# The affine step of the attention residual, moved from POOL in the output projection to DVE beside the projection of the values

## The chip, the cores and the metric

The kernel runs on one core of one Trainium2 chip. The metric is device time of that core in microseconds, from start to end of one execution; it is given as the median of several runs. Five engines matter: PE (TensorE, matmuls and transposes), DVE (VectorE), ACT (ScalarE), POOL (GpSimd) and SP (SyncE, which issues nearly all DMAs here). Each engine works through its own instructions in the order in which they stand.

## The reference

A trunk of two layers over 1024 tokens of width 1024. Layer 0 mixes with a state space model (`s5_mixer`), layer 1 with dilated attention; behind each mixer stand a residual with layer norm, a gated feed-forward network with a short convolution, and another residual with layer norm. The keys and values of the attention are projected from the output of layer 0.

```
def post_norm(x, f, gain, bias):
    return layer_norm(DN_ALPHA * x + f.astype(x.dtype), gain, bias)

for layer in range(DEPTH):
    mix = s5_mixer(h, ...) if layer < N_A_LAYERS else dilated_attention(h, w_q, w_out, rel_bias, kv_blocks)
    h = post_norm(h, mix, ln_gain[layer, 0], ln_bias[layer, 0])
    ffn = conv_glu_ffn(h, ffn_w_up[layer], ...)
    h = post_norm(h, ffn, ln_gain[layer, 1], ln_bias[layer, 1])
    if layer == N_A_LAYERS - 1:
        kv_blocks = shared_kv(h, attn_w_kv)
```

What is changed is where a part of one line is computed: the `* gain + bias` of the norm that ends layer 0, and the `DN_ALPHA *` of the residual that ends the attention. The attention reads `h` in another form, transposed, and gets gain and bias there by another way; the residual reads it token by token.

## The kernel before, in words

All matrices are in fp32 and each product is made of three matmuls (lines 88 to 90: high times high, high times low, low times high). For that every operand is split into a high part, by a cast on ACT (line 83, `CAST wh`, `CAST hT`), and a low part, by a subtraction on DVE (line 84, `wl`, `hT`). A weight tile is 128x1024 fp32 (512 KB): SP loads it into one of two buffers named `raw` (line 75), ACT and DVE split it into `wh` and `wl`.

A tensor of 1024x1024 is held as eight tiles `acc` of 128 tokens by 1024. At the end of layer 0 the function `after` normalizes each tile (line 129, mean and deviation only) and stores it to DRAM as `h1` (line 1556, `h<-acc` in the profile). For the matmuls the same tiles are transposed: `to_T` and `turn` let PE transpose blocks into PSUM (line 180, `tp`), and ACT (line 185) or DVE (line 183) write `tmp`, the block times gain plus bias, which is then split into `hT`. The tokens come in two halves, `hT[k][0]` and `hT[k][1]`, k from 0 to 7.

Then the values are projected. `values_first` does the first block for the token tiles j = 0 to 3, with the first half of `hT`, while PE still lacks the second. Behind it stand the transposes of the second half, and then, in `attention`, the same block for j = 4 to 7 and five more blocks. In `attention` the pool `ap` is opened, on memory that the tiles of layer 0 (`acc`, `tmp`, the weights of the values) held. For the first block, two of its four pairs of weights (k = 0 to 3) are kept from before; the other two (k = 4 to 7) are split anew into tiles of `ap`. The matmuls of these tiles are `v<-wh,hT` in the profile, and the copies of their results `vs<-v` (line 529), stored to `vscr`.

Behind the attention stands the output projection, `out_proj`, which is used by both layers. It takes the tokens in groups of three, three and two tiles; for each group it runs through eight weight tiles `in_w_out`. Before the matmuls of layer 1, SP loads two tiles `gb` (gain and bias, one row of DRAM broadcast to 128 partitions, line 156) and the eight tiles `acc` back from `h1` (line 1543, `acc<-h`). POOL multiplies each by the gain and adds the bias (lines 134 and 135). When a group's matmuls are done, DVE computes ALPHA times `acc` plus the product in PSUM (line 1489, `acc<-acc,wo`), and the norm follows.

A scheduler sets the order of the instructions on each engine, from its own forecast of their times. It works for the whole program but the state space model, so that a change at one place also moves instructions at others. A tile in a newly opened pool waits for all that used the memory under it.

Of the kernel before, what the change touches and what calls it, by code (L numbers as in the profile page):

```python
# [13 lines left out]
ALU = mybir.AluOpType  # L14
# [4 lines left out]
P = 128  # L19
# [5 lines left out]
ALPHA = (2.0 * 2) ** 0.25  # L25
# [448 lines left out]
def attn_bias_rows(net, pool, ps1):  # L474

    nc, a = net.nc, net.a
    rb = net.cp.tile([64, NG, 32], F32, "rb")
    nc.gpsimd.memset(rb[:], 0.0)
    nc.gpsimd.memset(rb[32:64], -1e30)
    for g in range(NG):  # L480
        nc.sync.dma_start(rb[0:32, g, 0:16], a["rel_bias"][:, g * 16 : g * 16 + 16])
    net.brow = net.dp.tile([NG, 16, LB], F32, name="brow")
    for g in range(NG):
        raw = pool.tile([P, 2, 512], F32, "s", "oh")
        nc.sync.dma_start(raw[0:64, 0, 0:LB], a["onehot"][:, g])
        ps = ps1.tile([P, 512], F32, "t", "bps")
        nc.tensor.matmul(ps[0:32, 0:LB], rb[:, g, :], raw[0:64, 0, 0:LB], start=True, stop=True)
        nc.scalar.copy(raw[0:16, 1, 0:LB], ps[0:16, 0:LB])
        nc.sync.dma_start(net.brow[g], raw[0:16, 1, 0:LB])


def attn_bias(net):

    net.bscr = []
    for g in range(NG):
        scr = net.dp.tile([16, P, LB], F32, name=f"bscr{g}")
        net.nc.gpsimd.dma_start(scr[:], net.brow[g].unsqueeze(1).broadcast_to([16, P, LB]))
        net.bscr.append(scr)
# [46 lines left out]
def attention(net, hT, ap, ws):  # L545
    nc = net.nc
    net.evn = 0
    for blk in range(2 * NG):
        if blk:
            ws = [net.wload(net.a["w_v"][blk, i], **({"pool": ap, "tag": "q"} if i < 3 else {})) for i in range(4)]  # L550
        else:
            ws = ws + [net.wload(net.a["w_v"][0, i], pool=ap, tag="q") for i in (2, 3)]
        for j in range(8) if blk else range(4, 8):
            ps = net.psA.tile([P, 512], F32, "mm", "v")
            st = ap.tile([P, 4, P], F32, "pt", "vs")
            value_tile(net, blk, j, hT, ws, ps[:], st[:])

    net.oscr = net.dp.tile([8, P, T], F32, name="oscr")
    nxt = Pair(net, 0, hT, ap)
    nxt.proj(0)  # L560
    for hp in range(8):
        pair = nxt
        for g in range(NG):
            if g:
                pair.proj(g)
            pair.scores(g)
        if hp < 7:
            nxt = Pair(net, hp + 1, hT, ap)
            nxt.proj(0)
        oT = pair.output()  # L570

    row = [[net.xp.tile([P, 2, 512], F32R, "x", "gT") for k in range(KT)] for _ in range(2)]
    for k in range(KT):
        if k < 7:
            raw = net.rawp.tile([P, T], F32, "raw", "oraw")
            nc.sync.dma_start(raw[:], net.oscr[k])
        else:
            raw = oT
        for hf in range(2):
            x = row[hf][k]  # L580
            net.split(raw[:, hf * 512 : hf * 512 + 512], x[:, 0, :], x[:, 1, :], nc.gpsimd if k < 7 else nc.vector)
    return [[row[hf][k] for hf in range(2)] for k in range(KT)]
# [885 lines left out]
    return gT  # L1468


def out_proj(net, w, gT, load, accp, hres, middle):

    nc = net.nc
    accs = []
    for tts in ((0, 1, 2), (3, 4, 5), (6, 7)):
        for tt in tts:
            accs.append(accp.tile([P, D], F32, "acc"))
            load(accs[tt], tt)
        pss = [net.psp.tile([P, D], F32, "mm", "wo") for _ in tts]
        for k in range(KT):  # L1480
            wh, wl = net.wload(w[k])
            for tt, ps in zip(tts, pss):
                g, q = gT[k][tt // 4], tt % 4
                lh, ll = (g[:, i, q * P : q * P + P] for i in range(2))
                for h in range(2):
                    sl = slice(h * 512, h * 512 + 512)
                    net.mm3(ps[:, sl], lh, ll, wh[:, sl], wl[:, sl], k == 0, k == KT - 1)
        for tt, ps in zip(tts, pss):
            nc.vector.scalar_tensor_tensor(
                out=accs[tt][:], in0=accs[tt][:], scalar=ALPHA, in1=ps[:], op0=ALU.mult, op1=ALU.add  # L1490
            )
            net.ln_apply(accs[tt])
            nc.sync.dma_start(hres[tt * P : tt * P + P, :], accs[tt][:])
        if 3 in tts:
            middle(accs)
    return accs


def program(tc, a, out):
    nc = tc.nc  # L1500
    with ExitStack() as ctx:
        net = Net(tc, ctx, a, out)
        net.persistent()
        net.dp = ctx.enter_context(tc.tile_pool(name="dp", bufs=1, space=DRAM))
        xp = net.xp = net.pool("xp", x=16)
        yT = [[None, None] for _ in range(KT)]
        with ExitStack() as c:
            cs = net.pool("s5c", c, c32=31, other=1)
            sp = net.pool("s5", c, s=11, w3=8, w2=3, u=3, Y=2, ms=2, r8=2, rq=1, other=1)
            psv, ps1 = net.pool("psv", c, PSUM, v=2), net.pool("ps1", c, PSUM, t=4)  # L1510
            s5 = S5(net, sp, cs, psv, ps1)
            s5.load_params()
            attn_bias_rows(net, sp, ps1)
            s5.run(xp, yT)

        net.weight_pools(4, 2)
        h1 = net.dp.tile([T, D], F32, name="h1")
        for l in range(2):
            if l == 1:
                with ExitStack() as c:  # L1520
                    gT = attention(net, hT, setup(net, c), V0)
            with ExitStack() as c:
                accp, tm = net.pool(f"acc{l}", c, acc=8), net.pool(f"tm{l}", c, t=4)
                hres = net.dp.tile([T, D], F32, name=f"hres{l}")
                half0 = []
                with ExitStack() as c2:
                    net.psp, net.tp = net.pool(f"ps{l}", c2, PSUM, mm=3, tp=2), "tp"
                    gp = net.pool(f"g{l}", c2, y=16)

                    def middle(accs):  # L1530
                        half0.extend(net.to_T(accs, 0, 2 * l, xp, tm))

                    if l == 0:
                        gT = glu(net, yT, tm, gp)
                        attn_bias(net)

                        def load(acc, tt):
                            nc.sync.dma_start(acc[:], a["x"][tt * P : tt * P + P, :])
                    else:
                        gb = net.load_gb(gp, 1, "y")  # L1540

                        def load(acc, tt):
                            nc.sync.dma_start(acc[:], h1[tt * P : tt * P + P, :])
                            net.ln_affine(acc, gb, nc.gpsimd)

                    accs = out_proj(net, a["w_out0" if l == 0 else "w_out1"], gT, load, accp, hres, middle)
                with ExitStack() as c2:
                    net.psp, net.tp = net.pool(f"pf{l}", c2, PSUM, s=6, tp=2), "tp"
                    fp = net.pool(f"f{l}", c2, xc=12, ws=5)
                    done, early = [], []  # L1550

                    def after(tt, acc):
                        done.append(acc)
                        if l == 0:
                            net.ln_apply(acc)
                            nc.sync.dma_start(h1[tt * P : tt * P + P, :], acc[:])
                            if tt == 4:
                                early.extend(net.to_T(done, 0, 1, xp, tm)[0])
                            return
                        if tt == 0:  # L1560
                            after.gb = net.load_gb(fp, 3, "xc")
                        net.ln_final(acc, after.gb, tt)
                        nc.sync.dma_start(out[tt * P : tt * P + P, :], acc[:])

                    net.ffn(l, accs, half0, xp, tm, fp, accp, hres, after)
                if l == 0:
                    with ExitStack() as c2:
                        net.psp, net.tp = net.pool("pv", c2, PSUM, mm=3, tp=2), "tp"
                        fp = net.pool("fv", c2, x=14)
                        hT = [[x, None] for x in early]  # L1570
                        V0 = values_first(net, hT, fp)
                        for k, t in enumerate(net.to_T(done, 1, 1, xp, tm)[0]):
                            hT[k][1] = t


def feature_tiles(w):
# [58 lines left out]
```

## Time and profile before

| | us |
|---|---|
| median of 3 runs (lowest, highest) | 3154.55 (3151.91, 3155.58) |
| the profiled execution | 3154.37 |
| its span, first to last instruction | 3152.4 |
| PE busy in the span | 2901.9 (92%) |
| DVE busy | 1929.7 (61%) |
| ACT busy | 1126.6 (36%) |
| POOL busy | 260.8 (8%) |

The profile is of one execution, and its places are given in us from the start of the span. The end of layer 0 and the first values lie at 1110 to 1180, the last pair of the attention and the output projection of layer 1 at 2200 to 2410. What lies outside the span is 3154.37 - 3152.4 = 2.0 us. PE is busy 92% of the span, so almost every wait of PE, and each stretch that it runs at a lower clock, is in the time.

### The profile page before, as it was taken

The numbers are of one execution on the slowest core, as the hardware profiler recorded it, in microseconds if no ns is written. First come the engines' busy times: TensorE is split into PE (matmuls) and PEld (weight loads), VectorE is DVE, ScalarE is ACT, GpSimd is POOL, SyncE is SP. The second block draws the span as 40 slices with busy tenths as digits, with TensorE's granted clock in tenths as the row PEclk, the third lists the DMA queues.
The fourth block names the chain that finished last, engine by engine and source line by source line (L and its number), as shares of the span: only waits on it lengthen the run. The fifth ranks groups of instructions, "written<-read, shape, count | busy, mean of one in ns | idle before, by whom it ended". The sixth has DMA issues, their size and how long they took to land.

```text
span 3152.4 us, 38280 instructions
## 1 busy us (share of the span) xinstructions
PE 2901.9 (92%) x13926; PEld 2374.7 (75%) x13926; DVE 1929.7 (61%) x3605; ACT 1126.6 (36%) x1977; POOL 260.8 (8%) x259
## 2 busy tenths in 40 slices
PE   4689989999989989999999999999688999998988
PEld 3668768888767768998777777777566788886766
DVE  8964687777688751113444444344457877767797
ACT  2433343333334431102433334333424433333442
POOL 8920000000100000000000000000250000001010
PEclk8889999999999999999999999999799999998999
DMA  5231532333653233326555556545443332328332
GB/s 176 59 122 60 174 104 105 112 109 112 249 179 107 89 102 113 107 68 164 148 151 146 134 140 156 141 130 144 137 170 137 111 107 107 107 101 336 98 101 67
DMA packets 189291, 408.11 MB, mean 129 GB/s; under 512 B 23984, under 2 KB 65696, under 8 KB 189104
## 3 DMA queue, kind: packets, MB, share of 16 engines
q1 hardware_dynamic: 180656, 373.16, 38.7%
q0 software_dynamic: 8448, 32.51, 2.8%
q8 instruction: 110, 1.80, 0.2%
q14 instruction: 77, 0.63, 0.1%
HBM read 249.79 MB, written 89.73 MB: 108 GB/s over the span
## 4 chain that ended last, share of the span: by engine, by line
PE 79%; DVE 8%; DMA 5%; POOL 4%; ACT 2%; issue 2%; SPq 1%; DVEq 0%; ACTq 0%; POOLq 0%
PE dn L398 13%; PE p L89 7%; PE p L88 7%; PE p L90 7%; PE qk L88 6%; PE qk L89 6%; PE qk L90 6%; PE o L810 3%; PE v L88 3%; PE v L90 3%; PE v L89 3%; PE t L800 2%; PE s L673 2%; DMA vs<-vs 1%; PE pa L88 1%
## 5 line engine op out<-in xcount | busy, mean ns | idle before, releaser
L398 PE MATMUL dn<-wh,ax 128*128 128x512 f32 x1408 | 396.5, 401 | 51.0 <-ACT ax L83 49.8
L84 DVE TENSOR_TENSOR wl<-raw,wh 128x1024 fp32r<-128x1024 f32 x174 | 221.7, 1275 | 280.8 <-ACT wh L83 280.7
L88 PE MATMUL p<-xc,wc 128*128 128x512 f32 x880 | 351.3, 400 | 16.6 <-DVE s L288 10.1
L83 ACT CAST wh<-raw 128x1024 fp32r<-128x1024 f32 x174 | 182.5, 1049 | 507.2 <-PE qk L89 155.1
L398 PEld LDWEIGHTS dn<-wh,ax 128*128 128x128 f32 x1408 | 269.0, 193 | 118.7 <-ACT ax L83 59.4
L90 PE MATMUL p<-xc,wc 128*128 128x512 f32 x880 | 348.1, 397 | 3.7 <-DVE wc L84 3.7
L89 PE MATMUL p<-xc,wc 128*128 128x512 f32 x880 | 351.2, 399 | 0.0
L88 PE MATMUL qk<-hT,wh 128*128 128x512 f32 x768 | 308.9, 402 | 10.4 <-DVE ql L611 10.4
L89 PE MATMUL qk<-hT,wh 128*128 128x512 f32 x768 | 308.5, 402 | 0.0
L90 PE MATMUL qk<-hT,wl 128*128 128x512 f32 x768 | 307.3, 400 | 0.0
L398 PE MATMUL dn<-wl,ax 128*128 128x512 f32 x704 | 228.9, 406 | 0.0
L88 PEld LDWEIGHTS p<-xc,wc 128*128 128x128 f32 x880 | 167.5, 190 | 60.2 <-ACT wc L83 20.5
L90 PEld LDWEIGHTS p<-xc,wc 128*128 128x128 f32 x880 | 166.3, 189 | 44.6 <-DVE wc L84 5.4
L89 PEld LDWEIGHTS p<-xc,wc 128*128 128x128 f32 x880 | 167.9, 191 | 39.3
L83 ACT CAST wc<-s 128x512 fp32r<-128x512 f32 x176 | 108.1, 621 | 238.6 <-PE p L90 228.9
L88 PEld LDWEIGHTS qk<-hT,wh 128*128 128x128 f32 x768 | 148.0, 193 | 41.7 <-DVE ql L611 12.4
L90 PEld LDWEIGHTS qk<-hT,wl 128*128 128x128 f32 x768 | 147.8, 192 | 29.7
L89 PEld LDWEIGHTS qk<-hT,wh 128*128 128x128 f32 x768 | 148.1, 193 | 28.9
L398 PEld LDWEIGHTS dn<-wl,ax 128*128 128x128 f32 x704 | 139.4, 198 | 31.4
L661 DVE CUSTOM_DVE_ANT_0 p<-s,bt 128x256 f32<-128x256 f32 (+1 forms) x384 | 119.2, 370 | 65.9 <-PE s L673 65.4
L88 PE MATMUL v<-wh,hT 128*128 128x512 f32 x384 | 153.7, 401 | 5.1 <-DVE tmp L183 4.8
L89 PE MATMUL v<-wl,hT 128*128 128x512 f32 x384 | 153.4, 400 | 0.0
(295 smaller groups left out, 5655.2 us busy)
## 6 DMA issues: line engine op xcount, KB each, us to landing
raw<-in_w_up SPq DMA_DIRECT2D x94, 512.0 KB, 3.5
qs<-qh SPq DMA_DIRECT2D x288, 128.0 KB, 2.4
vs<-vs SPq DMA_DIRECT2D x132, 256.0 KB, 3.5
raw<-in_w_out SPq DMA_DIRECT2D x48, 512.0 KB, 3.5
kl<-ql SPq DMA_DIRECT2D x192, 128.0 KB, 2.4
vs<-cv SPq DMA_DIRECT2D x44, 512.0 KB, 3.0
wd<-in_w_down POOLq DMA_DIRECT2D x44, 512.0 KB, 16.4
vs<-yv SPq DMA_DIRECT2D x38, 512.0 KB, 2.6
```

Of the source, the lines that this page charges most:

```text
L83: nc.scalar.copy(hi, x)
L84: (eng or nc.vector).tensor_tensor(out=lo, in0=x, in1=hi.bitcast(F32), op=ALU.subtract)
L88: nc.tensor.matmul(out, lh, rh, start=first, stop=False)
L89: nc.tensor.matmul(out, lh, rl, start=False, stop=False)
L90: nc.tensor.matmul(out, ll, rh, start=False, stop=last)
L398: nc.tensor.matmul(ps[i][h][:], l_, w[wi][:, h * 512 : h * 512 + 512], start=(f == 0 and l_ is ah and wi == 0), stop=(f == NF - 1 and l_ i ...
L661: nc.vector.tensor_tensor_reduce(out=out, in0=s, in1=b, scale=1.0, scalar=-3.0e38, op0=ALU.add, op1=ALU.max, accum_out=m)
L673: nc.tensor.matmul(out, qx[:, qs], kv[i], start=(i == 0), stop=(i == 1))
L800: nc.tensor.transpose(ps[:, i * P : i * P + P], b, net.ident[:])
L810: nc.tensor.matmul(o[64 * h : 64 * h + 64, oc], v[:, 64 * h : 64 * h + 64], pt[h], start=st, stop=sp_)
```

## The change: what it does

The affine step leaves `load` in the output projection, with its two loads of `gb`. It now stands at the end of layer 0, behind `values_first` and the transposes of the second half: gain and bias are loaded there, ACT multiplies both by ALPHA (2 instructions of 128x1024), DVE multiplies each of the eight `acc` tiles by the one and adds the other (16 instructions of 128x1024), and each tile is then stored to `h1`. The stores of `h1` that `after` made as soon as a tile was normalized go; their number, eight, stays. `out_proj` in layer 1 loads finished tiles and adds the product with a factor of 1.0 in place of ALPHA. The instruction on DVE there is the same.

```
-def out_proj(net, w, gT, load, accp, hres, middle):
+def out_proj(net, l, gT, load, accp, hres, middle):
     nc = net.nc
+    w = net.a[f"w_out{l}"]
...
             nc.vector.scalar_tensor_tensor(
-                out=accs[tt][:], in0=accs[tt][:], scalar=ALPHA, in1=ps[:], op0=ALU.mult, op1=ALU.add
+                out=accs[tt][:], in0=accs[tt][:], scalar=1.0 if l else ALPHA, in1=ps[:], op0=ALU.mult, op1=ALU.add
             )
...
-                        gb = net.load_gb(gp, 1, "y")
-
                         def load(acc, tt):
                             nc.sync.dma_start(acc[:], h1[tt * P : tt * P + P, :])
-                            net.ln_affine(acc, gb, nc.gpsimd)
-
-                    accs = out_proj(net, a["w_out0" if l == 0 else "w_out1"], gT, load, accp, hres, middle)
+
+                    accs = out_proj(net, l, gT, load, accp, hres, middle)
...
                         if l == 0:
                             net.ln_apply(acc)
-                            nc.sync.dma_start(h1[tt * P : tt * P + P, :], acc[:])
                             if tt == 4:
...
                         for k, t in enumerate(net.to_T(done, 1, 1, xp, tm)[0]):
                             hT[k][1] = t
+
+                        gb = net.load_gb(fp, 1)
+                        for g in gb:
+                            nc.scalar.mul(g[:], g[:], ALPHA)
+                        for tt, acc in enumerate(done):
+                            net.ln_affine(acc, gb, nc.vector)
+                            nc.sync.dma_start(h1[tt * P : tt * P + P, :], acc[:])
```

Where the scheduler put this shows in the built programs. The first place is DVE behind the first values, before the change: `tmp` are the transposed blocks of the second half, `hT` their low parts, and `wl` at the end the low part of the new weights for k = 4 and 5.

```order
L183 TENSOR_SCALAR tmp_8470<-tp_8480,lnT_59 128x512
L84 TENSOR_TENSOR hT_8469<-tmp_8470,hT_8469 128x512
L183 TENSOR_SCALAR tmp_8489<-tp_8499,lnT_59 128x512
L84 TENSOR_TENSOR hT_8479<-tmp_8470,hT_8479 128x512
L84 TENSOR_TENSOR hT_8488<-tmp_8489,hT_8488 128x512
L183 TENSOR_SCALAR tmp_8508<-tp_8518,lnT_59 128x512
L84 TENSOR_TENSOR hT_8498<-tmp_8489,hT_8498 128x512
L84 TENSOR_TENSOR hT_8507<-tmp_8508,hT_8507 128x512
L183 TENSOR_SCALAR tmp_8527<-tp_8537,lnT_59 128x512
L84 TENSOR_TENSOR hT_8517<-tmp_8508,hT_8517 128x512
L84 TENSOR_TENSOR hT_8526<-tmp_8527,hT_8526 128x512
L84 TENSOR_TENSOR hT_8536<-tmp_8527,hT_8536 128x512
```

After the change the same stretch of DVE begins with the same four instructions, and then goes on so, its middle and its end:

```order
L134 TENSOR_TENSOR acc_6469<-acc_6469,gb_8537 128x1024
L134 TENSOR_TENSOR acc_6555<-acc_6555,gb_8537 128x1024
L134 TENSOR_TENSOR acc_6641<-acc_6641,gb_8537 128x1024
L183 TENSOR_SCALAR tmp_8500<-tp_8510,lnT_59 128x512
L134 TENSOR_TENSOR acc_6727<-acc_6727,gb_8537 128x1024
...
L183 TENSOR_SCALAR tmp_8519<-tp_8529,lnT_59 128x512
L134 TENSOR_TENSOR acc_7673<-acc_7673,gb_8537 128x1024
...
L84 TENSOR_TENSOR hT_8528<-tmp_8519,hT_8528 128x512
L135 TENSOR_TENSOR acc_7673<-acc_7673,gb_8539 128x1024
L84 TENSOR_TENSOR wl_8593<-raw_8590,wh_8592 128x1024
```

All 16 affine instructions stand between the second split of `hT` (8471) and `wl`, the last one right before `wl`. Ten of them (seven multiplications, three additions) stand ahead of the last `tmp` (8519).

The second place is SP at the same time, after the change: the stores of the values, the loads of `gb`, the stores of `h1`, and the first loads of the attention behind them. Each store waits for DVE.

```order
L531 DMA vscr<-vs_8406 128x4x128 [waits DVE_49]
L156 DMA gb_8537<-in_ln 128x1024
L156 DMA gb_8539<-in_ln 128x1024
L531 DMA vscr<-vs_8434 128x4x128 [waits DMAHW3_49,Activation_49]
...
L1577 DMA h_1744<-acc_7410 128x1024 [waits DMAHW0_49,DVE_49]
L1577 DMA h_1744<-acc_7492 128x1024 [waits DMAHW1_49,DVE_49]
L1577 DMA h_1744<-acc_7591 128x1024 [waits DMAHW2_49,DVE_49]
L1577 DMA h_1744<-acc_7673 128x1024 [waits DMAHW3_49,DVE_49]
L873 DMA eye_1445_8583<-in_eye 128x128 [waits DMAHW4_49,DMAHW3_49,DMAHW5_49,DMAHW2_49,DMAHW6_49,DMAHW1_49,DMAHW7_49,DMAHW0_49,PE_49]
```

Before the change the eight stores of `h1` stood further up, among the loads for the feed-forward network and for the values. The third place is ACT at the cast of the new weights, after the change; DMAHW0 to DMAHW7 are the eight completion counters that SP's DMAs take in turn.

```order
L1574 ACTIVATE gb_8539<-gb_8539 128x1024 [waits DMAHW2_49]
L83 CAST hT_8499<-tmp_8500 128x512 [waits Activation_49]
L185 ACTIVATE tmp_8519<-tp_8520,lnT_59 128x512 [waits PE_49]
L83 CAST hT_8509<-tmp_8500 128x512 [waits DVE_49]
L83 CAST hT_8518<-tmp_8519 128x512 [waits Activation_49]
L83 CAST hT_8528<-tmp_8519 128x512 [waits DVE_49]
L83 CAST wh_8592<-raw_8590 128x1024 [waits DMAHW3_49,DMAHW2_49,DMAHW4_49,DMAHW1_49,DMAHW5_49,DMAHW0_49,DMAHW6_49,DVE_49,DMAHW7_49,PE_49,Activation_49]
```

The cast waits for counters of DMAs in both programs, for seven before and eight after. The counts that it waits for are those of DMAs on the memory of layer 0: before the change four stores of values and three of `h1`, which need nothing of the second half's splits; after it the eight stores of `h1`, the last of which waits for the last affine instruction (`acc_7673`). The order of PE in this stretch is the same as before.

## Rows read from the trace of the kernel before

**Rows 1.** The page's first part: busy us, share, instructions.

```profile
PE 2901.9 (92%) x13926; PEld 2374.7 (75%) x13926; DVE 1929.7 (61%) x3605; ACT 1126.6 (36%) x1977; POOL 260.8 (8%) x259
```

**Rows 2.** Stretches: length, busy us by engine (PE first), PE clock, DMA, GB/s.

```profile
1134.00:1180.00 46.00, 42.39 (x191) 34.09 (x191) 15.80 (x20) 14.17 (x20) 0.00 (x0) 0.96 0.38 116
...
2297.00:2320.00 23.00, 18.02 (x75) 14.27 (x75) 7.26 (x7) 5.33 (x6) 13.76 (x6) 0.96 0.71 274
...
2319.00:2322.00 3.00, 3.00 (x8) 1.99 (x8) 3.00 (x2) 0.81 (x1) 3.00 (x1) 0.50 0.33 53
...
2345.00:2350.00 5.00, 3.90 (x17) 3.21 (x18) 5.00 (x12) 2.08 (x6) 5.00 (x2) 1.00 0.39 105
```

**Rows 3.** Timeline of DVE at the first values: start, length, idle before.

```profile
1148.09 0.69 DVE L529 COPY vs<-v 128x512 f32<-128x512 f32 x1 [9.73 <-PE v L90]
...
1156.09 0.81 DVE L183 TENSOR_SCALAR tmp<-tp,lnT 128x512 f32<-128x512 f32 x1
1156.81 1.29 DVE L84 TENSOR_TENSOR hT<-tmp,hT 128x512 fp32r<-128x512 f32 x2
1158.01 0.81 DVE L183 TENSOR_SCALAR tmp<-tp,lnT 128x512 f32<-128x512 f32 x1
```

**Rows 4.** Timeline of PE at the values behind the transposes.

```profile
1160.89 0.66 PE L88 MATMUL v<-wh,hT 128*128 128x512 f32 x1 [1.25 <-DVE tmp L183]
...
1168.05 0.63 PE L88 MATMUL v<-wh,hT 128*128 128x512 f32 x2
1168.52 0.40 PE L89 MATMUL v<-wl,hT 128*128 128x512 f32 x1
...
1174.19 0.50 PE L88 MATMUL v<-wh,hT 128*128 128x512 f32 x1 [0.36 <-DVE vs L529]
```

**Rows 5.** Timeline of ACT there: a transposed block, the new weights.

```profile
1155.87 0.77 ACT L185 ACTIVATE tmp<-tp,lnT 128x512 f32<-128x512 f32 x1
...
1162.62 2.00 ACT L83 CAST wh<-raw 128x1024 fp32r<-128x1024 f32 x2 [1.11 <-DVE hT L84]
```

**Rows 6.** Timeline of DVE in layer 0's feed-forward network, an affine step.

```profile
870.24 2.35 DVE L134 TENSOR_TENSOR acc<-acc,gb 128x1024 f32<-128x1024 f32 x2
872.51 1.22 DVE L135 TENSOR_TENSOR acc<-acc,gb 128x1024 f32<-128x1024 f32 x1
```

**Rows 7.** Scaling of gb on ACT, by line: ns min, median, max.

```profile
L419 ACT ACTIVATE gb<-gb x4: 1058/1061/1062, 836.1 to 2852.2; 128x1024 f32<-128x1024 f32 x4
```

**Rows 8.** Landing of the eight stores of h1, line 1556.

```profile
DMA to landing us min/median/max: 2.6/2.9/6.6
```

**Rows 9.** Landing of the two loads of gb at 2299, line 156.

```profile
DMA to landing us min/median/max: 3.8/4.5/5.2
```

**Rows 10.** Timeline of SP at the output projection of layer 1.

```profile
2299.05 0.81 SPq L156 DMA_DIRECT2D gb<-in_ln  x2
2299.90 5.03 SPq L1543 DMA_DIRECT2D acc<-h  x8
```

**Rows 11.** The chain of waits there: start, length, what.

```profile
2306.10 11.30 DMA raw<-in_w_out
2317.49 1.05 ACT wh L83
```

**Rows 12.** Timeline of PE there, its waits.

```profile
2318.59 1.65 PE L88 MATMUL wo<-wh,gT 128*128 128x512 f32 x3 [4.92 <-ACT wh L83]
...
2339.28 0.47 PE L88 MATMUL wo<-wh,gT 128*128 128x512 f32 x1 [1.02 <-DVE acc L1489]
2346.10 0.50 PE L89 MATMUL wo<-wl,gT 128*128 128x512 f32 x1 [1.58 <-DVE wl L84]
2380.07 0.50 PE L89 MATMUL wo<-wl,gT 128*128 128x512 f32 x1 [1.82 <-DVE wl L84]
```

**Rows 13.** Groups by line, 1150 to 1176: busy us, mean ns, idle before.

```profile
L84 DVE TENSOR_TENSOR wl<-raw,wh 128x1024 fp32r<-128x1024 f32 x4 | 4.8, 1220 | 7.4 <-ACT wh L83 7.4
```

**Rows 14.** Groups by line, 2297 to 2350.

```profile
L84 DVE TENSOR_TENSOR wl<-raw,wh 128x1024 fp32r<-128x1024 f32 x9 | 19.9, 2224 | 23.4 <-ACT wh L83 23.4
```

## The prediction

> **What bounds the kernel now.** I read the page's busy times first, then the stretches, the timelines of PE, DVE, ACT and SP at the two places that the change touches, and last the chain of waits there. PE is busy 92% of the span, POOL 8% [rows 1]: time is won or lost only where PE waits or runs at its lower clock. So the question at both places is what PE waits for, and how long.
>
> At the output projection of layer 1, PE is busy 18.0 of the 23 us from 2297 to 2320, while the DMAs move 274 GB/s [rows 2]. SP issues the two loads of gb at 2299.05 and behind them the eight loads of acc, until 2304.9 [rows 10]. The next weight tile, issued at 2306.10, lands only 11.30 us later [rows 11], and PE waits 4.92 us for its cast [rows 12]. Then PE's granted clock is 0.50, the 1.2 GHz level [rows 2].
>
> At the end of layer 0, the second half's transposes run through DVE, one block every second step, and PE's values begin at 1160.89, when DVE's last block is out of PSUM [rows 4]. From there to 1174 PE has no wait over 0.36 us. DVE is busy 15.8 of the 46 us from 1134 to 1180 [rows 2]; that it has room is clear, but the room lies ahead of 1154, while the values of the first half run (one wait alone is 9.73 us, [rows 3]).
>
> **The change part by part.** 1) The values. Sixteen affine instructions on DVE: two in a row take from 870.24 to 872.51, so 1.135 us each [rows 6], 18.2 us in all. The order puts them behind the second split of the second half. That split begins at 1156.81 and lasts 0.6 us ((1158.01 - 1156.81) / 2, [rows 3]), so DVE could begin the first multiplication at 1157.4. It needs gb: the loads stand behind the third store of values, whose copy ends at 1148.8 [rows 3], and land 3.8 to 5.2 us after their issue [rows 9], by 1154.4; ACT scales gb behind the block that it begins at 1155.87 [rows 5], in 1.06 us [rows 7], so by 1157.7. I take 1157.7 as the start.
>
> From there DVE has the 16 affine instructions (18.2), two blocks at 0.72 (1156.81 - 1156.09, [rows 3]) and six splits at 0.6, together 23.2 us, and ends at 1180.9. In that sum ten affine instructions, one block and four splits (11.4 + 0.7 + 2.4) come before the last block, which ends at 1172.9. PE's values wait for it as they do now, because their PSUM pool opens when it is done: they begin at 1173.1 and not at 1160.9. The 24 matmuls up to the new weights take 7.2 us (1168.05 - 1160.89, [rows 4]), to 1180.3.
>
> There the second wait begins. The cast of the new weights waits for all eight stores of h1. The last is issued some 0.3 us behind the last addition and takes 2.9 us, the median of the eight stores now [rows 8]: 1184.1. The cast takes 1.05 (as at 2317.49, [rows 11]), wl 1.22 [rows 13]: 1186.4. The first matmul with wl begins at 1168.52 now [rows 4], so PE comes 17.9 us later. It has just waited 4.9 us by this sum (1180.3 to 1185.2), as long as the wait in [rows 12], and after that one its clock was 0.50. There the matmuls stand 0.43 us apart in place of 0.23; I take 10 of them, 2.0 us. The values cost 19.9 us.
>
> What else is issued there: the two loads of gb and the scaling on ACT (2.1 us) lie beside DVE's work and are in the start above. Behind the waiting stores on SP stand eye, mask, the bias tiles and the first two loads of the next block's weights. These move by some 20 us as well, as does the PE work that needs them, so I take nothing. The cover is that PE still has 70 matmuls of the first block to do (16 us) when they start; without it, a late load is a wait of a few us. The old stores of h1 stood in SP's queue among loads that nothing waited for at that time: nothing.
>
> Bounds. From below, a store that lands in 2.6 us and no lower clock: 17.6 us. From above, 6.6 us for the store (the slowest of the eight, [rows 8]; the last four are issued within 5 us and may queue), a gb that is 3 us late because the broadcast shares the DMAs, and 3 us of clock: 27 us.
>
> 2) The output projection. The 16 instructions of POOL go, and 1 MB of loads ahead of the 4 MB of acc. SP needs 0.85 us less to issue (2299.90 - 2299.05, [rows 10]), and the tile that PE waits for stands behind 9 loads in place of 11, at a mean of 274 GB/s or more [rows 2]: 1 MB is 2.6 to 3.8 us. So PE's wait of 4.92 shrinks by 3.1 to about 1.8 us. A wait of 1.58 us left the clock at 1.00 [rows 2, 12], so the slow stretch goes: some 15 matmuls at 0.43 in place of 0.23, 2.9 us. Behind it PE waits 1.02 us for DVE at the change of groups [rows 12], because DVE's split was long under POOL; I count 0.7 of it. Of the 1.58 us at 2346 I count nothing, since a like wait of 1.82 us comes at 2380 [rows 12], when POOL is done. Together 6.7 us. The bounds are 2.6 (the MB alone, no clock) and 10.7 (all of 4.92, 3.2, 1.0 and 1.6).
>
> DVE's wl takes 2.224 us here and 1.220 at the values [rows 13, 14]: while POOL runs, the subtraction is nearly twice as long. The Trainium skill (SBUF — State Buffer, the part on who interferes with whom) says that DVE and POOL share one pair of ports, and that the later of two instructions blocks fully. By that rule the nine splits give back 9 x 1.0 = 9 us; if each of these were in PE's path, the gain here would be 9 us higher. The rows on PE's waits decide otherwise: it waited 2.6 us for DVE in that stretch [rows 12].
>
> 3) Elsewhere the scheduler moved instructions too: on ACT and DVE in the last pair of the attention, in the third group of the projection, and in the second feed-forward network. The trace does not price an order; I take 0 with 4 us to both sides.
>
> The sum: 3154.4 + 19.9 - 6.7 = 3167.6 us, from the profiled execution (3154.37, which is 0.2 us from the median of the runs). So some 0.4% slower.
>
> **The rivals.** a) It is costlier: the eight stores queue behind each other, gb comes late, PE drops its clock twice, and the projection, which still loads 4 MB of acc ahead of its weights, keeps most of its wait. For it: the loads of acc are slow by just such a queue. Against: a store is issued only every 1.1 us or more. With 25 for the values and 4 for the projection: 3175.
>
> b) Not slower, by the room on DVE: it is idle for 30 of the 46 us, and the affine step fits in. If it ran beside PE's values of the first half, only the gain would stay: 3154.4 - 6.7 = 3147.7. It decides at the place where PE's first matmul of the second half stands: if that comes by 1167, gain and loss are even. Against: the built order, and that the four tiles of the second half may be changed only behind their transposes. The Trainium skill (Perfetto Trace Analysis, Optimizing Scalar/DVE Operations) advises to take work off DVE when that engine is saturated. It is not saturated here, so by this rule the move to DVE costs nothing and the sum would be rival b's; the rows on who waits for DVE speak against it.
>
> c) The projection gives back all that it can (10.7, with 4 more from the new order behind it), and the values cost their least, 17.6: 3157. That is no change which can be measured. It needs both ends at once.
>
> **How the numbers follow.** Chances: the forecast 0.60 (its own range 3162 to 3173), a 0.25, c 0.11, b 0.04. What can be told from no change is about 0.2%, 6.3 us, so slower begins at 3160.9: the forecast and a lie beyond it, with a little of them short of it. Faster 0.04, within 0.10, slower 0.86. Range 3158 to 3178.
>
> **What would show it.** In the new profile, PE's first values of the second half begin near 1173; a wait of PE for ACT's wh stands near 1185, with a DMA h<-acc ahead of it in the chain; DVE is dense from 1157 to 1181. At the projection, PE's wait for wh is under 2.5 us with no stretch at 0.50 behind it, wl takes 1.22 throughout, and POOL does nothing. I would be wrong if values begin before 1167, if the cast does not wait for the stores, or if the new order in the second feed-forward network moves the time by more than 4 us.

## The result and the profile after

| | median us | runs | ratio to before, 95% interval |
|---|---|---|---|
| before | 3153.23 | 4 | |
| changed | 3168.89 | 4 | 1.0051 [1.0034, 1.0068] |
| changed, on another chip | 3174.23 (before there 3155.91) | 6 | 1.0046 [1.0033, 1.0059] |

The ratios and intervals are those on record with the runs; the ratio of the two medians can be another by up to 0.0012 (1.0058 in the last line). Two executions far from all others, 5750.93 us in E2 and 9362.95 us in E5, stand in no median and no ratio here.

The change makes the kernel 0.5% slower. The forecast was 3167.6 us, a ratio of 1.0042. The profiled execution took 3169.26 us, 14.9 more than that of before. The first line of its page, which answers to [rows 1]: POOL has lost its 16 instructions, DVE has gained 16, and PE is as busy as it was.

```profile
PE 2904.6 (92%) x13926; PEld 2378.6 (75%) x13926; DVE 1937.1 (61%) x3621; ACT 1127.0 (36%) x1979; POOL 217.3 (7%) x243
```

To see where the time goes, the program is cut at five landmarks of PE, and the length of each stretch is compared with before. The cuts are the starts of the first transpose of layer 0's second half, of the last matmul of the values, of the first and last matmul of layer 1's output projection, and of the last matmul of all. The first column is how much later the first cut comes.

| us against before | until the transposes | values (256.2) | attention (887.5) | projection (106.5) | rest (736.9) | sum |
|---|---|---|---|---|---|---|
| changed | -2.5 | +21.1 | +4.9 | -6.7 | -2.1 | +14.7 |
| changed, again (E9) | +6.5 | +22.0 | +3.7 | -6.2 | -4.5 | +21.6 |
| E1 blocks first | -0.8 | +22.6 | +6.8 | -8.0 | +0.8 | +21.2 |
| E2 half early | +2.6 | +10.6 | +5.5 | -7.9 | -0.5 | +10.2 |
| E3 all early | -0.5 | -0.2 | +2.4 | -7.0 | -4.5 | -9.8 |
| E3 again (E10) | -2.5 | -0.7 | +6.4 | -7.4 | -4.8 | -9.0 |
| E4 values alone | +2.5 | +20.9 | +8.2 | -0.8 | -6.7 | +24.0 |
| E5 no POOL | +5.2 | -0.6 | +6.2 | -4.2 | -3.6 | +3.0 |
| E6 no gb | +6.1 | -0.6 | +3.2 | -6.7 | -1.9 | +0.2 |
| E7 neither | -1.5 | +0.1 | +5.3 | -7.1 | -4.2 | -7.3 |
| E8 late loads | +4.3 | +1.2 | +5.0 | -10.8 | -1.7 | -1.9 |
| E8 again (E11) | +2.8 | -0.1 | +5.5 | -9.5 | -2.1 | -3.3 |

Two columns carry the change: the values and the projection. They are the same, within 2 us, in all profiles that have the same instructions there. The other columns move by several us for all, E5 too, whose PE, DVE, ACT and SP have exactly the instructions and order of before; they are how executions differ, so no cause is sought for them in the change. The profiled execution of before had the shortest attention of all, which is why every other row shows a loss there.

**At the values.** PE's timeline, which answers to [rows 4]. Places in this trace are 2.5 us earlier than in before's up to here (the first transpose comes at 1150.85; in before's timeline of PE its row is the following).

```profile
1153.33 1.03 PE L180 MATMUL tp<-ident,acc 128*128 128x128 f32 x8
```

And the changed kernel's:

```profile
1150.85 1.03 PE L180 MATMUL tp<-ident,acc 128*128 128x128 f32 x8
...
1159.00 1.12 PE L180 MATMUL tp<-ident,acc 128*128 128x128 f32 x4 [1.48 <-ACT tmp L185]
1170.49 0.80 PE L88 MATMUL v<-wh,hT 128*128 128x512 f32 x1 [10.37 <-DVE tmp L183]
...
1182.64 1.22 PE L88 MATMUL v<-wh,hT 128*128 128x512 f32 x2 [4.04 <-ACT wh L83]
1183.91 0.79 PE L89 MATMUL v<-wl,hT 128*128 128x512 f32 x1
...
1192.83 0.50 PE L88 MATMUL v<-wh,hT 128*128 128x512 f32 x1 [1.12 <-DVE vs L529]
```

There are two new waits: 10.37 us for DVE's last transposed block, and 4.04 us for the cast of the new weights. DVE's timeline between them ([rows 3] before) has no gap: the last block stands at 1169.63, behind ten affine instructions, and the last addition at 1177.23.

```profile
1155.14 3.50 DVE L134 TENSOR_TENSOR acc<-acc,gb 128x1024 f32<-128x1024 f32 x3
1158.56 0.81 DVE L183 TENSOR_SCALAR tmp<-tp,lnT 128x512 f32<-128x512 f32 x1
...
1169.63 0.81 DVE L183 TENSOR_SCALAR tmp<-tp,lnT 128x512 f32<-128x512 f32 x1
...
1177.23 1.22 DVE L135 TENSOR_TENSOR acc<-acc,gb 128x1024 f32<-128x1024 f32 x1
```

The chain of waits shows what the cast stood for: the last addition, the last store of h1, the cast.

```profile
1177.31 1.15 DVE acc L135
1178.47 2.67 DMA h<-acc
1181.55 1.05 ACT wh L83
```

Behind both waits PE runs at the lower clock. The stretches (length, busy us of PE, PEld, DVE, ACT, POOL, then PE's clock, DMA share, GB/s) answer to [rows 2]; the last two are the projection.

```profile
1131.50:1177.50 46.00, 31.35 (x139) 25.20 (x138) 26.56 (x30) 10.21 (x16) 0.00 (x0) 0.81 0.31 111
...
1182.60:1185.60 3.00, 2.92 (x6) 1.91 (x7) 2.36 (x2) 0.94 (x1) 0.00 (x0) 0.50 0.27 57
1185.60:1188.60 3.00, 3.00 (x8) 2.33 (x8) 0.00 (x0) 0.00 (x0) 0.00 (x0) 0.50 0.72 206
...
2330.00:2336.00 6.00, 6.00 (x28) 4.95 (x28) 1.20 (x1) 0.00 (x0) 0.00 (x0) 1.00 1.03 415
2339.50:2342.50 3.00, 2.94 (x7) 2.23 (x8) 2.45 (x2) 1.05 (x2) 0.00 (x0) 0.51 0.22 35
```

**At the projection** ([rows 10, 11, 12, 14] before): PE's waits, then SP's loads of acc, the chain, and DVE's group of wl.

```profile
2339.55 1.65 PE L88 MATMUL wo<-wh,gT 128*128 128x512 f32 x3 [2.32 <-ACT wh L83]
...
2362.75 0.51 PE L89 MATMUL wo<-wl,gT 128*128 128x512 f32 x1 [0.24 <-DVE wl L84]
```

```profile
2322.61 3.79 SPq L1542 DMA_DIRECT2D acc<-h  x8
```

```profile
2327.14 11.22 DMA raw<-in_w_out
2338.46 1.05 ACT wh L83
```

```profile
L84 DVE TENSOR_TENSOR wl<-raw,wh 128x1024 fp32r<-128x1024 f32 x11 | 13.4, 1223 | 26.2 <-ACT wh L83 26.2
```

The wait for the weights is 2.32 us in place of 4.92, wl takes 1.22 us in place of 2.22, and the lower clock behind the wait is still there, but shorter.

### The profile page after: what moved, and what is told of

Read it like the earlier page. It is cut to its first block, busy times and chain, and to the rows that moved or that the text cites. A ratio compares the mean times of both kernels' runs of the same rounds, so it can differ in the third digit from the quotient of the medians.

```text
span 3167.1 us, 38274 instructions
## 1 busy us (share of the span) xinstructions
PE 2904.6 (92%) x13926; PEld 2378.6 (75%) x13926; DVE 1937.1 (61%) x3621; ACT 1127.0 (36%) x1979; POOL 217.3 (7%) x243
## 4 chain that ended last, share of the span: by engine, by line
PE 53%; DVE 5%; DMA 3%; ACT 1%; SPq 1%; issue 1%; DVEq 0%; ACTq 0%
PE dn L398 7%; PE qk L88 6%; PE qk L89 6%; PE qk L90 6%; PE p L90 4%; PE p L88 4%; PE p L89 4%; PE o L810 3%; PE v L88 2%; PE v L90 2%; PE v L89 2%; PE t L800 2%; PE s L673 2%; DMA qs<-qh 1%; DMA raw<-in_w_out 1%
## 5 line engine op out<-in xcount | busy, mean ns | idle before, releaser
L84 DVE TENSOR_TENSOR wl<-raw,wh 128x1024 fp32r<-128x1024 f32 x174 | 212.7, 1223 | 285.9 <-ACT wh L83 281.1
L88 PE MATMUL p<-xc,wc 128*128 128x512 f32 x880 | 351.6, 400 | 14.7 <-DVE s L288 8.8
## 6 DMA issues: line engine op xcount, KB each, us to landing
vs<-vs SPq DMA_DIRECT2D x132, 256.0 KB, 3.5
```

Source lines behind the costliest of these rows:

```text
L84: (eng or nc.vector).tensor_tensor(out=lo, in0=x, in1=hi.bitcast(F32), op=ALU.subtract)
L88: nc.tensor.matmul(out, lh, rh, start=first, stop=False)
```

## The experiments

Each ratio is against before on the same chip, whose median was 3157.4 us beside E1 to E4, 3156.87 beside E5 to E8 and 3155.91 beside E9 to E11. The expectations count from 3153.2, so a time is to be read by its distance from before.

Theory A: behind the transposes, the values pay for DVE's whole chain, because the new weights go into memory that is free only when the last store of h1 has landed. Theory B: they pay because the blocks stand behind affine instructions (the first wait). Theory C: the loss is in the scheduler's new order elsewhere. For the projection, theory D: the gain is 1 MB less in a full queue of DMAs; theory E: it is DVE freed of POOL.

**E1, the blocks first.** The line ahead of the loop is new; `last_block` is what `turn` issues on DVE.

```
+                        with tc.issue_after(net.last_block.ins):
                             for tt, acc in enumerate(done):
                                 net.ln_affine(acc, gb, nc.vector)
```

> The changed kernel, but on DVE the affine step stands behind the last transposed block of the second half (tmp, k=7), so that PE's first values do not wait for it. Theory A (the loss is set by the second wait: all 16 affine instructions and the last store of h1 must be done before the new weights may be cast): PE begins its values near 1160, but then waits for the cast until 1182 as now; the total stays at that of the changed kernel, less the one stretch at the lower clock that goes with the first wait (2.4 us): 3166 to 3169 us. Theory B (the loss is the first wait, 10.4 us, because the blocks stand behind affine instructions): this gives it back, 3157 to 3160 us.

Measured: 3177.83 us, 20.4 above the 3157.4 of before on that chip, 1.0066 [1.0042, 1.0089]; the changed kernel is 15.7 above, and 18.3 in E9. PE's timeline, DVE's, and one stretch:

```profile
1160.18 0.76 PE L88 MATMUL v<-wh,hT 128*128 128x512 f32 x1 [1.00 <-ACT tmp L187]
1185.73 1.22 PE L88 MATMUL v<-wh,hT 128*128 128x512 f32 x2 [18.23 <-ACT wh L83]
```

```profile
1159.95 9.16 DVE L134 TENSOR_TENSOR acc<-acc,gb 128x1024 f32<-128x1024 f32 x8
...
1172.58 8.03 DVE L135 TENSOR_TENSOR acc<-acc,gb 128x1024 f32<-128x1024 f32 x7
```

```profile
1160.00:1163.00 3.00, 2.81 (x7) 2.27 (x8) 3.00 (x4) 2.16 (x5) 0.00 (x0) 0.53 0.03 5
```

The first wait is gone and the second has grown by as much and more: 18.23 us. The values take 278.8 us, 1.4 more than in the changed kernel; 0.9 of that is the last store, which lands after 3.59 us here and after 2.67 there. So theory B falls. The total lies above what theory A gave as well (13 to 16 us above before), but its interval reaches down to 13. The 2.4 us that I expected back did not come: the stretch from 1160 to 1163 runs at 0.53 here too, and before's first 24 matmuls [rows 4] take 7.2 us, more than 24 at the full clock would (0.23 us apart, 5.5). A slow stretch stood there before the change too; it did not belong to the new wait.

**E2, half of it early; E3, all of it early.** Loads of gb, scaling and the affine step go in front of the matmuls of the first values. In E2 the second half's tiles stay behind the transposes; in E3 they are written to new tiles.

```
     ws = [net.wload(...) for i in range(4)]
+    with net.tc.issue_after(net.normed.ins):   # behind the last norm of layer 0
+        beside(range(4))                       # tiles 0 to 3, in place
     for j in range(4):
         ...
+        if j == 0:                             # E3 alone
+            with net.tc.issue_after(net.copied.ins):
+                beside(range(4, 8))            # into fp.tile(..., "x", "aff")
```

> The changed kernel, but gain and bias are loaded before the first values and the affine step of the four tiles of the first half stands on DVE beside the values of the first half; the four tiles of the second half stay where the change put them. Theory A: 8 of the 16 instructions leave the chain behind the transposes, 8 x 1.135 = 9.1 us: PE's first values begin near 1162, the cast of the new weights near 1172; 3168.9 - 9.1 = 3160 us (3158 to 3162). Theory B: the first wait shrinks by the instructions ahead of the last block, 7 of 10, 7.9 us: 3161. Theory C (the time was lost elsewhere, by the order the scheduler made of the attention and the second feed-forward network): no change, 3168 us.

Measured: 3162.95 us, 5.6 above before (6.8 written), 1.0023 [1.0008, 1.0038].

```profile
1166.89 0.76 PE L88 MATMUL v<-wh,hT 128*128 128x512 f32 x1 [4.65 <-DVE tmp L183]
1178.40 1.22 PE L88 MATMUL v<-wh,hT 128*128 128x512 f32 x2 [4.14 <-ACT wh L83]
```

The values lose 10.6 in place of 21.1 us: half the chain, half the loss. That speaks against theory C; A and B forecast nearly the same time here. The first matmul comes some 2 us later than I wrote (1164.3 in before's places), since three multiplications still stand ahead of the last block.

> As the one before, but the second half's four tiles are also done beside the values of the first half, written into four free tiles in place of their own, so that the transposes may still read them. All 16 instructions are in DVE's idle time there (4.0 + 9.7 + 5.6 us in the changed kernel, for 18.2). Theory A: the values cost nothing, or up to 1.5 us where gain and bias land too late for all of it to fit; what is left is the gain at the output projection: 3153.2 - 6.7 + 1 = 3147.5 us (3145 to 3151), faster than both. Rival: with DVE full PE waits for its copies of the first values (three PSUM buffers), 5 us or more: 3153 and above. Theory C: 3168.

Measured: 3151.62 us, 5.8 below before (5.7 written), 0.9979 [0.9965, 0.9994]. DVE's timeline beside the first values, and PE's first matmul of the second half:

```profile
1133.07 4.62 DVE L1583 TENSOR_TENSOR acc<-acc,gb 128x1024 f32<-128x1024 f32 x4
1137.61 3.49 DVE L1584 TENSOR_TENSOR acc<-acc,gb 128x1024 f32<-128x1024 f32 x3
1141.02 0.68 DVE L529 COPY vs<-v 128x512 f32<-128x512 f32 x1
...
1147.30 4.62 DVE L1584 TENSOR_TENSOR aff<-aff,gb 128x1024 f32<-128x1024 f32 x4
1151.84 0.68 DVE L529 COPY vs<-v 128x512 f32<-128x512 f32 x1
```

```profile
1160.42 0.66 PE L88 MATMUL v<-wh,hT 128*128 128x512 f32 x1 [1.25 <-DVE tmp L183]
```

The same 16 instructions on the same engine cost nothing here: PE waits 1.25 us, as in [rows 4], and the values take 256.0 us, as before. DVE copies the first results at 1141 and not at once, and PE does not wait for it: from its first matmul of the values to the first transpose of the second half it takes 23.9 us, as before. With E1 to E3 theory A stands, and C falls.

How much of the chain is the memory, and how much DVE's own order, is not shown. In the changed kernel `wl`, which PE needs as well, stands on DVE behind all 16 instructions; DVE is idle for 4.18 us ahead of it, while the last store lands and the cast runs. So these two are at most 4.2 us of the loss, and the rest is DVE's work ahead of `wl`. No run puts the new weights into other memory, which would tell whether `wl` could stand further up.

```profile
1182.62 2.36 DVE L84 TENSOR_TENSOR wl<-raw,wh 128x1024 fp32r<-128x1024 f32 x2 [4.18 <-ACT wh L83]
```

**E4, the values alone.** The changed kernel with POOL's step and the loads of gb back in the projection; the residual gets the affine step twice.

```
+                        gb = net.load_gb(gp, 1, "y")
...
+                            net.ln_affine(acc, gb, nc.gpsimd)
```

> The changed kernel, with the step on POOL and its two loads of gb put back into the output projection as well, so that the affine step is done twice (the output is another). It is the change at the values alone. If the gain at the projection is 6.7 us, as the two traces show from the start of its matmuls on (23.6 to 16.6 us later than before), this is slower than the changed kernel by that: 3175 to 3177 us. If the shift there was an accident of the order, it stays at 3169.

Measured: 3179.69 us, 22.3 above before, 1.0067 [1.0044, 1.0090]. The projection takes 105.7 us, 5.9 more than in the changed kernel, and PE's wait is back:

```profile
2349.59 1.65 PE L88 MATMUL wo<-wh,gT 128*128 128x512 f32 x3 [4.35 <-ACT wh L83]
```

The totals alone do not tell the two kernels apart, since their intervals overlap.

**E5, E6, E7, the projection alone.** The kernel before without POOL's step (E5), without the loads of gb (E6), without both (E7).

```
-                        gb = net.load_gb(gp, 1, "y")                  # E6, E7
...
-                            net.ln_affine(acc, gb, nc.gpsimd)         # E5, E7
+                            net.ln_affine(acc, (acc, acc), nc.gpsimd) # E6
```

> The kernel before, without POOL's 16 affine instructions in the output projection (the residual is then not scaled); the two loads of gb stay, and PE, DVE, ACT and SP have the same instructions in the same order as before. Theory D (the gain at the projection is the 1 MB of gb ahead of the weights in a queue of DMAs that is full): PE's wait for the cast of the weights stays near 4.9 us with the stretch at the lower clock behind it, and only the waits for DVE go: 1 to 2.5 us faster than before, from the first matmul of the projection to the start of its second group 40 to 41 us (before 42.2, the changed kernel 37.0). Theory E (the gain is DVE freed of POOL: wl of 3.3 us delays the weight buffer and so the next load): most of the gain is here already, 37 to 38 us from first matmul to second group.

> The kernel before, without the two loads of gb; POOL multiplies and adds each tile with itself, the same 16 instructions of the same size (other numbers). Theory D: PE's wait for the cast falls from 4.9 to 2.3 us, as in the changed kernel, and the part from first matmul to second group takes 38 to 39.5 us; some 3 to 4 us faster than before. Theory E: the wait stays above 4 us, 41 to 42 us.

> The kernel before, without POOL's 16 instructions and without the loads of gb (the residual is not scaled): the gain at the projection alone, with the values as before. Theory: 6.7 us faster than before (5 to 9), 3146.5 where before has 3153; the part from first matmul to second group 35 to 37 us, as in the changed kernel. If that gain belonged to the order made for the changed kernel and not to the step that is gone, it is less than 3 us.

The first group is counted from the projection's first matmul to the first of the second group.

| | ratio | wait for wh us | first group us | projection us |
|---|---|---|---|---|
| before | | 4.92 | 42.2 | 106.5 |
| E5 | 0.9995 [0.9985, 1.0005] | 4.80 | 39.9 | 102.3 |
| E6 | 0.9985 [0.9973, 0.9996] | 1.82 | 36.0 | 99.8 |
| E7 | 0.9978 [0.9967, 0.9988] | 2.19 | 37.0 | 99.4 |
| changed | 1.0051 [1.0034, 1.0068] | 2.32 | 37.0 | 99.8 |

PE's waits and the group of wl in E5, without POOL:

```profile
2329.22 1.65 PE L88 MATMUL wo<-wh,gT 128*128 128x512 f32 x3 [4.80 <-ACT wh L83]
...
2352.85 0.50 PE L89 MATMUL wo<-wl,gT 128*128 128x512 f32 x1 [0.24 <-DVE wl L84]
```

```profile
L84 DVE TENSOR_TENSOR wl<-raw,wh 128x1024 fp32r<-128x1024 f32 x7 | 8.6, 1226 | 27.6 <-ACT wh L83 27.6
```

DVE is free of POOL at once (1.23 us for wl), and yet the long wait stays: theory E falls for it. What went are PE's short waits for DVE (1.02 at the change of groups, 1.58 down to 0.24). In E6 POOL still runs and the wait is 1.82 us: theory D. PE's clock behind it (same columns as above):

```profile
2324.28 0.97 PE L88 MATMUL wo<-wh,gT 128*128 128x512 f32 x3 [1.82 <-ACT wh L83]
```

```profile
2324.00:2327.00 3.00, 2.43 (x9) 1.72 (x10) 2.71 (x2) 1.27 (x2) 3.00 (x2) 1.00 0.14 26
```

That is why E6's first group is 2 us under the lower end that I wrote: the slow stretch, which E7 and the changed kernel still have in part, is gone. E5 and E6 do not add up to E7 (4.2 and 6.7 against 7.1 us). The clock has a part in that: E6 has no slow stretch, E7 has one behind its wait of 2.19 us (0.53 over 3 us). The rest is not taken apart.

E7 has before's values and the whole gain at the projection, so that gain belongs to the step that is gone and not to the order made for the changed kernel. E5's total cannot be told from before's; its 4.2 us are seen in the trace alone.

**E8, late loads.** E3, and in the projection each group's loads of acc stand behind its fourth weight tile on SP.

```
+            if l and k == 3:
+                with net.tc.issue_after(net.loaded.ins):
+                    for tt in tts:
+                        load(accs[tt], tt)
```

> All 16 affine instructions beside the values of the first half, as in the run that was faster than before, and in the output projection of layer 1 each group's loads of acc stand behind the fourth weight tile of that group on SP, in place of all eight ahead of the weights. By theory D the wait of 2.3 to 2.6 us for the weights and the stretch at the lower clock behind it go (1.5 to 2 us): 4 us faster than that run, some 10 us faster than before (0.3%). If the loads then delay the later weights instead, there is no difference from that run.

Measured: 3151.66 us, 0.9980 [0.9970, 0.9990], the same as E3; the 4 us that I expected beyond E3 do not show in it. SP's timeline has three loads of acc and not eight ahead of the next weights:

```profile
2309.68 1.28 SPq L1552 DMA_DIRECT2D acc<-h  x3
2314.21 31.71 SPq L75 DMA_DIRECT2D raw<-in_w_out  x8
```

PE's first group takes 32.8 us, with no wait for wh at all. But the medians cannot tell that from E3. So three kernels ran again on one chip: E9 the changed kernel, E10 is E3, E11 is E8.

> The changed kernel once more, beside the two versions below on one chip. All theories: 0.4 to 0.6% slower than before. In the stretches: 20 to 22 us lost between the transposes of the second half and the end of the values, 6 to 7 us won from the first to the last matmul of the projection; the stretches that hold the same instructions in the same order (the attention up to the last pair) differ from before by no more than the 6 us by which a kernel with before's order differed there.

> All 16 affine instructions beside the values of the first half, acc loaded ahead of the weights at the projection. 0.2% faster than before, as the first time (0.9979).

> The same with each group's loads of acc behind its fourth weight tile. The trace showed 4.3 us less from the first matmul of the projection to the second group (37.1 to 32.8 us), but the medians did not differ. If the 4.3 us are in the time, this is 0.1 to 0.15% faster than the run beside it; if they are given back behind it, in the projection's later groups or the feed-forward network, it is the same within 0.05%.

E9: 3174.23 us, 1.0046 [1.0033, 1.0059], with the stretches as expected. E10: 3147.85 us, 0.9966 [0.9954, 0.9978]. E11: 3146.80 us, 0.9963 [0.9951, 0.9976]. E11's first group is 3.9 us shorter than E10's (32.8 and 36.7), its later groups 1.9 us longer (0.5 in E8 against E3), where the weights of the last group now stand behind its loads:

```profile
2383.40 0.73 PE L88 MATMUL wo<-wh,gT 128*128 128x512 f32 x2 [0.89 <-ACT wh L83]
...
2388.23 0.73 PE L88 MATMUL wo<-wh,gT 128*128 128x512 f32 x2 [1.00 <-ACT wh L83]
```

The 2 us that are left are too few for these medians, which lie 1.05 us apart. Both E3 and E8 beat the kernel before, by 0.2 to 0.4%, and the changed one by 0.7 to 0.9%.

## Why the prediction was right

**The chain at the values** came out step by step. With 2.5 us added to the places of the new trace, the affine step starts at 1157.6 (written 1157.7), PE's first values at 1173.0 (1173.1), the cast at 1184.0 (1184.1), and the first matmul with wl at 1186.4 (1186.4), 17.9 us later than before. E1 shows that I had the right wait: I wrote both, and took the sum from the second alone.

**What lies behind it** was under-sized: 2.0 us written, 3.2 measured (21.1 - 17.9). The lower clock is 2.5 of them: the stretch at 0.50 lasts some 6 us, 12 matmuls 0.2 us late each. The other 0.8 is a term that I put at nothing, the next block's weights. Their `wl` now ends so late that DVE's copy right behind it makes PE wait 1.12 us, where it waited 0.36 [rows 4]:

```profile
1190.95 1.23 DVE L84 TENSOR_TENSOR wl<-raw,wh 128x1024 fp32r<-128x1024 f32 x1 [5.96 <-ACT wh L83]
1192.09 0.68 DVE L529 COPY vs<-v 128x512 f32<-128x512 f32 x1
```

My upper bound for the values was added up wrongly as well: 17.9 + 3.7 + 3 + 3 is 27.6 and not 27.

**The projection** gave 6.7 us, as written, but its terms were not those, so that the number is right is luck. The megabyte is 2.6 us and not 3.1 (4.92 - 2.32). The reason is in the queue: from the first issue to the landing of the weight tile it took 18.35 us before ([rows 10, 11]: 2306.10 + 11.30 - 2299.05) and 15.75 after (first load at 2322.61, landing at 2338.36), 2.60 less, while the tile's own landing stayed at 11.2. While the queue is full it moves 415 GB/s, and 1.05 MB at that rate are 2.5 us; the mean of 274, from which I took the upper end of 3.8 us, is that of a stretch which is partly idle. The Trainium skill (DMA: Bandwidth & Descriptors, Where 436 GB/s comes from) lets loads from HBM be bound by some 358 GB/s, and the ports by 435; this trace disagrees with the first and is near the second.

The slow clock did not go, though I had named that as a sign: I wrote 2.9 us for it and 1.6 came (5.25 us of the first group, less 2.60 and 1.02). A wait of 2.32 us was left and not one of 1.8. In E1 and E2, which have the same projection, waits of 1.52 and 1.72 us were left, the clock stayed at 1.00 behind them, and the gain was 8.0 and 7.9 us; why the waits differ is not shown. And the waits for DVE gave more: 1.02 and 1.34 in place of 0.7. There I had argued that the 1.58 us would stay, because a like wait comes later without POOL. The changed kernel and E5 both show 0.24: that step was wrong. The errors cancelled: 0.5 and 1.3 us too much, 1.7 too little.

The Trainium skill (SBUF — State Buffer, Who interferes with whom) has a DVE instruction with two SBUF inputs contend with a POOL instruction that reads SBUF. E5 agrees: wl, which has two such inputs, goes from 2.22 to 1.23 us when POOL's step goes. Only 4.2 us of the nine that this frees reach PE. The two waits for DVE are 2.4 of them; the stretch at the lower clock is shorter too (the second 3 us behind the wait run at 0.78, before at 0.50).

**Elsewhere** I took 0 with 4 us to both sides. The profiles give +0.3 in sum (-2.5, +4.9, -2.1), but +5.7 in E9, and E5's attention, with nothing moved, is 6.2 us longer than before's. So no price of the order shows, and 4 us to both sides was less than the spread of single executions.

**The rivals.** Rival b, the room on DVE, described a real possibility at the wrong place: E3 is that kernel, at 0.9979 and 0.9966 where b's 3147.7 would be 0.9979. The built order excluded it for this change, as I wrote. For rival a the stores would have had to queue, but the last one landed in 2.67 us; for rival c the projection would have had to give 14.7 us, and it gave 6.7. My chance of 0.86 for slower was more than the 0.85 of its two parts.

## What to carry to other kernels

Work put on an engine that has room (here 30 of 46 us) still costs what it makes others wait for: look for what stands behind it on that engine and for who needs the memory that it holds, since removing the wait you see first can just move PE to the next. If the same work can be issued where the engine waits anyway, it can cost nothing, as in E3, which took four more tiles for the results. For a transfer behind a full queue, price the bytes ahead of it at the queue's full rate, and take the time from the queue's first issue, not from the transfer's own landing.

## What the runs showed of the hardware that was not expected

Executions of one program differ more between profiles than the medians suggest: attention took 887.5 to 893.7 us for the same instructions in the same order (before and E5), and the first transposes came 2.5 us earlier to 6.5 us later than in before's profile. A gain of 2 us in a stage is seen in a trace and lost in a median. And a short wait can change what follows. At the first wait for `wh` in the projection, waits of 1.52 (E1), 1.72 (E2) and 1.82 us (E6) left the clock at 1.00, while those of 1.89 (E10), 2.19 (E7), 2.32 (changed), 2.47 (E9), 2.60 us (E3) and more were followed by 0.50 to 0.58 over 3 us. That holds for this place alone: in E1 one of 1.00 us, behind transposes with gaps of their own, was followed by 0.53. E2's wait, then E10's and the stretch behind it:

```profile
2334.00 0.98 PE L88 MATMUL wo<-wh,gT 128*128 128x512 f32 x3 [1.72 <-ACT wh L83]
```

```profile
2318.78 1.43 PE L88 MATMUL wo<-wh,gT 128*128 128x512 f32 x3 [1.89 <-ACT wh L83]
```

```profile
2318.70:2321.70 3.00, 2.92 (x7) 2.00 (x8) 2.45 (x2) 1.08 (x2) 0.00 (x0) 0.56 0.25 26
```
